# State-space sines one piece later, accumulated low parts from the 21st chunk with the negated copy first, and tiles moved in SBUF

## The chip, the cores and the metric

The kernel runs on one core of a Trainium2 chip. The time is the device time of one execution in microseconds; several executions are summed up by their median. TensorE (PE) multiplies, VectorE (DVE), ScalarE (ACT) and GpSimd (POOL) do the elementwise work, SyncE (SP) issues most DMAs; each takes its instructions strictly in the order in which they stand in the program.

## What is computed

One block of a decoder on 512 tokens with 2048 channels, all in float32:

```python
h = h + token_mixer(rmsnorm(h, norm_tok))     # one projection w_in to u, v, gates, merge gates;
                                              # state space, short convolution, w_glu, w_ssm_out,
                                              # w_conv_out, sigmoid merge, w_o
h = h + conv_ffn(rmsnorm(h, norm_ffn))        # w_up to 2 x 5632, convolution of 3 taps, gelu, w_down
return rmsnorm(h, norm_final)
```

The state space `s5_scan` has 32 pairs of groups; for each the kernel makes cosines and sines of phases, a product, two scans, a turn back and another product.

## The kernel before

**Products in three parts.** A float32 product is made of three `float32r` products: with hi the rounded value and lo what is left, it is hi·xh + hi·xl + lo·xh. The weights stand still in TensorE (128 x 128 at a time), the activations move, 512 columns (all tokens) or 256 (half of them). `products` issues the three matmuls for each of 8 blocks of a chunk: lines 161 (hi with xh), 162 (hi with xl) and 163 (lo with xh).

**Chunks.** The weights come in chunks of 128 x 1024 (8 blocks). The list `flat` holds all chunks in order, each with its unit (one output tile of 128 channels). A chunk passes through `load_to` (SyncE loads it to one of 3 `wraw` buffers) and `prep_to`, which makes its two parts in one of 3 `whi` and one of 3 `wlo` buffers. ScalarE copies to `whi` (line 138). The low part is made in one of two ways: by VectorE, `wlo = wraw - whi` (line 125), or, for units with `acc` set, ScalarE writes the rounded and negated `wraw` to `wlo` (line 141), and a DMA from GpSimd's queue adds `wraw` to it in SBUF (line 142). `acc` is set for the chunks from `flat[6:]` to the 20th merge unit, and of those a chunk goes to VectorE all the same when the count of background pieces left is 2 modulo 3.

**Order around a chunk.** When the products of chunk i stand in the program, `after(i)` issues, in this order: the two parts of chunk i + 3 (its buffers become free with chunk i), stores that were put off (`later`), loads up to chunk i + 5, then the next background pieces, then the hooks, then the unit's own end (`done`).

**Background pieces.** `bg_pieces(n)` makes three pieces for each n, which are taken one per chunk from the chunk 12 on, two per chunk in every fourth merge unit: `first` (the sum `ssm_y`, the sines `ssm_trig(n-1)`, the product `ssm_out`, the turn `ssm_turn(n-3)` on GpSimd, the scan of one half), `second` (the scan of the other half), `third` (a load, the product `ssm_bu`, the phases `ssm_phase(n)` on VectorE, lines 443 to 446, which write `ph`). `ssm_trig` is three ScalarE instructions (lines 452 to 454) that read `ph` and write `cs`; the scan and the turn read `cs`.

**The stages.** Chunks 0 to 15 are the state-space input u (each u tile is split to `uh` and `ul`, one buffer each, and stored by SyncE); 16 to 63 are the convolution's v, c and b gates; 64 to 127 the merge gates ("merges"); then w_conv_out (moving tile kh/kl), w_glu (xh/xl), w_ssm_out (kh/kl) and w_o (xh/xl), all with 512 columns. The two first units of w_up, `ua` and `ub`, move x2h/x2l with 512 columns; the other 43 pairs of w_up units (`Pair`) are computed with 7 chunks instead of 8 by sums of weights, with 256 columns: chunks 0, 3, 4, 5 move x2h/x2l, chunks 1 and 2 th/tl, chunk 6 the tile `xga`. w_down moves th/tl and x2h/x2l with 512 columns, its last 4 output tiles in two halves of 256.

**Where tiles lie.** Pools stack their tiles from the left or the right end of SBUF, so an address follows from the sizes of all tiles before it. Only its place within 256 bytes matters here:

| tile | before | with the change |
|---|---|---|
| whi, wlo | 192 | 192; 128 in units with `off` |
| xh, xl | 192 | 192 |
| kh, kl | 224 | 192 |
| x2h, x2l, xga | 224 | 128 |
| th, tl | 192 | 128 |
| ust and bst (state space) | 224 | 192 |

Of the kernel before, what the change touches and what calls it, by code (L numbers as in the profile page):

```python
# [16 lines left out]
P = 128  # L17
# [9 lines left out]
HALVES = (slice(0, T // 2), slice(T // 2, T))  # L27
SPLIT = 4

MAGIC = 12582912.0  # L30
# [18 lines left out]
class Unit:  # L49
# [7 lines left out]
    def __init__(self, chunks, xs, done, pre=None, bg=0, hooks=None, cols=slice(0, T), late=False, post=None):  # L57
        self.chunks, self.xs, self.done, self.pre, self.bg = chunks, xs, done, pre, bg
        self.hooks, self.cols, self.late, self.post = hooks or {}, cols, late, post
        self.total = sum(c[1] for c in chunks)  # L60
        self.k, self.ps = 0, None
        self.acc = False


@with_exitstack
def block_kernel(ctx: ExitStack, tc: tile.TileContext, a: dict):
# [5 lines left out]
    dpool = ctx.enter_context(tc.tile_pool(name="dpool", bufs=1, space=DRAM))  # L72
    psm = ctx.enter_context(tc.tile_pool(name="psm", bufs=3, space=PSUM))
    ctx.enter_context(tc.manual_schedule())

# [52 lines left out]
    def prep_to(n, late=False):  # L128
        while n_["prep"] < min(n, len(flat)):
            i = n_["prep"]  # L130
            load_to(i + 1)
            u, c = flat[i]
            w = slice(0, u.chunks[c][1] * P)
            raw = raws.pop(i) if i in raws else u.raw(c)
            hi = wpool.tile([P, 1024], F32R, tag="whi", name="whi")
            lo = wpool.tile([P, 1024], F32R, tag="wlo", name="wlo")
            preps[i] = (hi, lo)
            nc.scalar.activation(hi[:, w], raw[:, w], AF.Copy)  # L138
            if getattr(u, "acc", False) and len(bg) % 3 != 2:

                nc.scalar.activation(lo[:, w], raw[:, w], AF.Copy, scale=-1.0)
                nc.gpsimd.dma_start(lo[:, w], raw[:, w], accum_op=ALU.add)
                n_["prep"] += 1
                continue
            los.append((lo[:, w], raw[:, w], hi[:, w].bitcast(F32)))
            if not late:
                lo_all()
            n_["prep"] += 1
# [69 lines left out]
    def kd_chunks(w, n):  # L218
        return [(w[2 * n], 8), (w[2 * n + 1], 8)]
# [288 lines left out]
    def bg_pieces(n):  # L508

        def ok(p):  # L510
            return 0 <= p < NPAIR

        def quad(m):
            return m % 4 == 3 and ok(m)

        def first():
            if quad(n - 6):
                ssm_y((n - 6) // 4)
            if ok(n - 1):
                ssm_trig(n - 1)  # L520
            if quad(n - 5):
                ssm_out((n - 5) // 4)
            if ok(n - 3):
                ssm_turn(n - 3)
            if ok(n - 2):
                ssm_scan(n - 2, 0)

        def second():
            if ok(n - 2):
                ssm_scan(n - 2, 1)  # L530

        def third():
            if quad(n - 4):
                ur_load((n - 4) // 4)
            if ok(n - 1):
                ssm_bu(n - 1)
            if ok(n):
                ssm_phase(n)
                ssm_load(n + 1)
        return [first, second, third]  # L540
# [108 lines left out]
    add(*merges)  # L649
    for u, _ in flat[6:]:  # L650
        u.acc = u not in merges[20:]
# [6 lines left out]
    def start():  # L658
# [11 lines left out]
        raw = wpool.tile([P, 1024], F32, tag="wraw", name="wraw")  # L670
        hi = wpool.tile([P, 1024], F32R, tag="whi", name="whi")
        lo = wpool.tile([P, 1024], F32R, tag="wlo", name="wlo")
        half = [slice(0, 512), slice(512, 1024)]
# [173 lines left out]
    def sumsq(i, cols=slice(0, T)):  # L847
        h = hrow(i, cols)
        if i == 0:
            nc.scalar.activation(acc[:, cols], h, AF.Square)  # L850
            return
        ff["sq"] = fx("sq", (P, T), bufs=2)
        nc.scalar.activation(ff["sq"][:, cols], h, AF.Square)  # L853
# [42 lines left out]
    def gate_open():  # L896
        xctx.close()
        ff["gp"] = ctx.enter_context(tc.tile_pool(name="gp", bufs=1, side="left"))
        ff["pss"] = ctx.enter_context(tc.tile_pool(name="pss", bufs=5, space=PSUM))
        ff["TH"], ff["TL"] = (gt(t, 1, (P, KS, T), F32R) for t in ("th", "tl"))  # L900
        ff["pad"] = gt("ap", 1, (P, T + 2))
# [87 lines left out]
    class Pair:  # L989

        late = True
        pre = post = None

        def __init__(self, G):
# [106 lines left out]
    pairs = {G: Pair(G) for G in range(1, NG)}  # L1101
    ua, ub = (Unit(kd_chunks(a["w_up"], KF * r + ORDER[0]), xs2, f(ORDER[0])) for r, f in ((0, fa_done), (1, fb_done)))
    ua.pre = gate_open
    ua.hooks = {0: [f_sums, lambda: t_sums(KD - 1), lambda: s_first(1)], 1: [f_spread, t1_split, lambda: s_copy(1)]}
# [66 lines left out]
    for b_, (k0, kn) in enumerate(DOWN):  # L1171
# [3 lines left out]
        def down(n, **kw):  # L1175
            return Unit([(a["w_down"][n][:, k * P:(k + m) * P], m) for k in range(k0, k0 + kn, m)],
                        lambda k, k0=k0: xsd(k0 + k), dn_done(n, last, **kw), late=bool(kw), **kw)

        dns = [down(n) for n in range(KD - SPLIT if last else KD)]
        if not last:  # L1180
# [3 lines left out]
            for j in range(n1):  # L1184
                dns[3 + j].hooks.setdefault(0, []).append(lambda k=k1 + j: dg_split(k))
        add(*dns)
        if last:
# [5 lines left out]
            ends[SPLIT + 2].post = lambda: out_store(0, 4, 8)  # L1193
            add(*ends)

# [69 lines left out]
```

## Time and profile before

| | us |
|---|---|
| median of 3 runs | 2573.52 (2573.16 to 2574.19) |
| the profiled execution's own time | 2575.06 |
| its span, first to last instruction | 2573.3 |
| TensorE busy | 2520.0 (98%) |
| VectorE busy | 1670.1 (65%) |
| ScalarE busy | 1058.2 (41%) |
| GpSimd busy | 575.3 (22%) |
| granted TensorE clock, mean | 0.993 |

Times in rows are microseconds from the start of the span. Matmuls are pipelined: the mean ns of one in a row is longer than the distance from one start to the next, so the pace is read as the length of a stretch over the count of matmuls in it. PE is TensorE's matmuls, PEld its weight loads, SPq the queue of SyncE.

### The profile page before, as it was taken

What the parts mean: (1) busy time and instruction counts of PE and PEld (TensorE: products, weight loads), DVE (VectorE), ACT (ScalarE), POOL (GpSimd) and SP (SyncE); (2) the same over time, 40 slices, a digit from 0 to 9 for tenths busy, and PEclk for the clock granted to TensorE, in tenths of its full rate; (3) what the DMA queues carried; (4) which work ended last, traced back from release to release, by engine and by line L of the source; (5) the groups of instructions that cost most, each with busy time, mean ns of one, the idle gap of its engine ahead of it and who ended that gap; (6) DMA issues with size and microseconds to landing.
All of it is one profiled execution on the core that took longest, in us unless ns stands there. A gap on an engine that the chain in (4) does not pass through costs nothing.

```text
span 2573.3 us, 36516 instructions
## 1 busy us (share of the span) xinstructions
PE 2520.0 (98%) x14616; PEld 2204.6 (86%) x14616; DVE 1670.1 (65%) x1967; ACT 1058.2 (41%) x1343; POOL 575.3 (22%) x443
## 2 busy tenths in 40 slices
PE   9899999989999999999999999999999999999997
PEld 7678887767888888888999999999999988888887
DVE  6388889999323455446777777787777753333335
ACT  6344444444223433334544544555554432222222
POOL 2167777676202121110000000000000000000011
PEclk9999999999999999999999999999999999999998
DMA  7876777677445334443666666666666663434335
GB/s 218 240 175 182 192 205 192 172 188 192 141 149 191 123 127 141 145 144 123 169 182 179 169 164 177 190 185 172 170 181 175 195 238 112 126 112 123 97 92 152
DMA packets 151066, 424.70 MB, mean 165 GB/s; under 512 B 18032, under 2 KB 26352, under 8 KB 150896
## 3 DMA queue, kind: packets, MB, share of 16 engines
q1 hardware_dynamic: 121648, 330.88, 40.7%
q0 software_dynamic: 22176, 80.75, 16.5%
q10 hardware_dynamic: 7072, 10.74, 1.2%
q8 instruction: 114, 1.87, 0.3%
q14 instruction: 56, 0.46, 0.1%
HBM read 300.67 MB, written 40.89 MB: 133 GB/s over the span
## 4 chain that ended last, share of the span: by engine, by line
PE 86%; DMA 4%; issue 4%; DVE 3%; POOL 2%; ACT 1%; SPq 0%; ACTq 0%; DVEq 0%; POOLq 0%
PE mm L163 18%; PE mm L161 18%; PE mm L162 17%; PE sr L1021 11%; PE sr L1019 11%; PE sr L1020 11%; DMA wlo<-wraw 2%; POOL pt L94 1%; DVE wlo L125 1%; PE py L492 1%; DMA wraw<-in_w_in 1%; POOL xx L94 0%; DMA wraw<-wraw 0%; POOL xx L484 0%; PE w L461 0%
## 5 line engine op out<-in xcount | busy, mean ns | idle before, releaser
L125 DVE TENSOR_TENSOR wlo<-wraw,whi 128x1024 fp32r<-128x1024 f32 (+1 forms) x384 | 467.4, 1217 | 387.8 <-ACT whi L138 387.5
L138 ACT ACTIVATE whi<-wraw 128x1024 fp32r<-128x1024 f32 (+1 forms) x452 | 454.0, 1006 | 514.7 <-PE mm L162 389.1
L163 PE MATMUL mm<-xh,wlo 128*128 128x512 f32 x1344 | 529.9, 394 | 28.7 <-DMA wlo<-wraw 26.3
L161 PE MATMUL mm<-xh,whi 128*128 128x512 f32 x1344 | 529.6, 394 | 5.8 <-ACT whi L97 5.8
L162 PE MATMUL mm<-xl,whi 128*128 128x512 f32 x1344 | 527.7, 393 | 0.2 <-DVE xl L102 0.2
L1021 PE MATMUL sr<-x2h,wlo 128*128 128x256 f32 x1376 | 386.8, 281 | 1.4 <-DVE wlo L125 1.4
L1019 PE MATMUL sr<-x2h,whi 128*128 128x256 f32 x1376 | 385.5, 280 | 0.6 <-ACT whi L138 0.6
L1020 PE MATMUL sr<-x2l,whi 128*128 128x256 f32 x1376 | 382.8, 278 | 0.0
L163 PEld LDWEIGHTS mm<-xh,wlo 128*128 128x128 f32 x1344 | 254.9, 190 | 89.6 <-DMA wlo<-wraw 32.2
L161 PEld LDWEIGHTS mm<-xh,whi 128*128 128x128 f32 x1344 | 254.9, 190 | 66.2 <-issue 6.1
L162 PEld LDWEIGHTS mm<-xl,whi 128*128 128x128 f32 x1344 | 254.9, 190 | 55.0 <-DVE xl L102 1.4
L1021 PEld LDWEIGHTS sr<-x2h,wlo 128*128 128x128 f32 x1376 | 258.3, 188 | 2.2 <-DVE wlo L125 2.0
L1019 PEld LDWEIGHTS sr<-x2h,whi 128*128 128x128 f32 x1376 | 258.8, 188 | 0.8 <-ACT whi L138 0.8
L1020 PEld LDWEIGHTS sr<-x2l,whi 128*128 128x128 f32 x1376 | 258.8, 188 | 0.0
L163 PE MATMUL mm<-x2h,wlo 128*128 128x512 f32 (+1 forms) x528 | 197.8, 375 | 0.9 <-DVE wlo L125 0.9
L161 PE MATMUL mm<-x2h,whi 128*128 128x512 f32 (+1 forms) x528 | 198.5, 376 | 0.1
L162 PE MATMUL mm<-x2l,whi 128*128 128x512 f32 (+1 forms) x528 | 197.3, 374 | 0.0
L1021 PE MATMUL sr<-th,wlo 128*128 128x256 f32 x688 | 194.8, 283 | 0.9 <-DVE wlo L125 0.9
L1020 PE MATMUL sr<-tl,whi 128*128 128x256 f32 x688 | 194.7, 283 | 0.0
L1019 PE MATMUL sr<-th,whi 128*128 128x256 f32 x688 | 194.6, 283 | 0.0
L855 POOL TENSOR_TENSOR acc<-acc,sq 128x512 f32<-128x512 f32 (+1 forms) x31 | 37.6, 1214 | 655.0 <-ACT sq L853 655.0
L125 DVE TENSOR_TENSOR wlo<-r,whi 128x1024 fp32r<-128x1024 f32 x88 | 107.5, 1222 | 46.7 <-ACT whi L138 46.7
(246 smaller groups left out, 4534.3 us busy)
## 6 DMA issues: line engine op xcount, KB each, us to landing
wraw<-in_w_in SPq DMA_DIRECT2D x127, 512.0 KB, 4.3
r<-in_w_up SPq DMA_DIRECT2D x88, 512.0 KB, 6.1
xgb<-in_w_up SPq DMA_DIRECT2D x84, 512.0 KB, 5.5
wraw<-in_w_down SPq DMA_DIRECT2D x104, 384.0 KB, 3.3
wlo<-wraw POOLq DMA_DIRECT2D x68, 512.0 KB, 5.7
wraw<-wraw POOLq DMA_DIRECT2D x43, 512.0 KB, 9.6
wraw<-in_w_o SPq DMA_DIRECT2D x32, 512.0 KB, 3.6
r<-r POOLq DMA_DIRECT2D x22, 512.0 KB, 4.5
```

The source lines that it names most:

```text
L94: eng.tensor_tensor(o, x, y, op=ALU.mult)
L125: nc.vector.tensor_tensor(o, x, y, op=ALU.subtract)
L138: nc.scalar.activation(hi[:, w], raw[:, w], AF.Copy)
L161: nc.tensor.matmul(u.ps[:, u.cols], hi[:, w], xh, start=first, stop=False)
L162: nc.tensor.matmul(u.ps[:, u.cols], hi[:, w], xl, start=False, stop=False)
L163: nc.tensor.matmul(u.ps[:, u.cols], lo[:, w], xh, start=False, stop=last)
L492: nc.tensor.matmul(py[32 * q:32 * q + 32, :], cblk[:, p, j, :], xx[p][:, j], start=(j == 0), stop=(j == 1))
L855: nc.gpsimd.tensor_tensor(acc[:, cols], acc[:, cols], ff["sq"][:, cols], op=ALU.add)
L1019: nc.tensor.matmul(ps, hi[:, w], xh, start=(c < 4 and j == 0), stop=False, skip_group_check=c >= 4)
L1020: nc.tensor.matmul(ps, hi[:, w], xl, start=False, stop=False, skip_group_check=c >= 4)
L1021: nc.tensor.matmul(ps, lo[:, w], xh, start=False, stop=j == 7, skip_group_check=c >= 4)
```

## The change

Three things. First, `acc` is set from `flat[20:]` on, so that chunks 6 to 19 get their low part from VectorE, and where the low part is accumulated the negated copy to `wlo` stands ahead of the copy to `whi`. Second, `ssm_trig(n-1)` moves from piece `first` to the start of piece `second`. Third, tiles move: `whi` and `wlo` are 64 elements longer (`WT`), and a unit's `off` (0, or `SHIFT` = 48 elements, 192 bytes) says where in them its 1024 columns begin; `ua`, `ub` and all w_down units have the shift. A pool `edge` of 32 bytes at the right end, an `edge` tile of 192 bytes ahead of th and tl, and a single `sq` buffer of 528 instead of two of 512 elements set the places in the table above. In distances, 512-column products have weights and moving tile at the same place within 256 bytes throughout, and so do the 256-column products of w_down's last tiles; in the 43 pairs the weights lie 64 bytes beyond the moving tile.

```diff
+WT = 1024 + 64
+SHIFT = 48
...
-        self.acc = False
+        self.acc, self.off = False, 0
...
+    edge = ctx.enter_context(tc.tile_pool(name="edge", bufs=1, side="right"))
+    edge.tile([P, 8], F32, tag="edge", name="edge")
...
-            hi = wpool.tile([P, 1024], F32R, tag="whi", name="whi")
-            lo = wpool.tile([P, 1024], F32R, tag="wlo", name="wlo")
+            hi = wpool.tile([P, WT], F32R, tag="whi", name="whi")
+            lo = wpool.tile([P, WT], F32R, tag="wlo", name="wlo")
+            hi, lo = (x[:, u.off:u.off + 1024] for x in (hi, lo))
             preps[i] = (hi, lo)
-            nc.scalar.activation(hi[:, w], raw[:, w], AF.Copy)
             if getattr(u, "acc", False) and len(bg) % 3 != 2:

                 nc.scalar.activation(lo[:, w], raw[:, w], AF.Copy, scale=-1.0)
+                nc.scalar.activation(hi[:, w], raw[:, w], AF.Copy)
                 nc.gpsimd.dma_start(lo[:, w], raw[:, w], accum_op=ALU.add)
                 n_["prep"] += 1
                 continue
+            nc.scalar.activation(hi[:, w], raw[:, w], AF.Copy)
...
         def first():
             if quad(n - 6):
                 ssm_y((n - 6) // 4)
-            if ok(n - 1):
-                ssm_trig(n - 1)
...
         def second():
+            if ok(n - 1):
+                ssm_trig(n - 1)
             if ok(n - 2):
                 ssm_scan(n - 2, 1)
...
-    for u, _ in flat[6:]:
+    for u, _ in flat[20:]:
         u.acc = u not in merges[20:]
...
-        ff["sq"] = fx("sq", (P, T), bufs=2)
+        ff["sq"] = fx("sq", (P, T + 16))[:, :T]
...
         ff["pss"] = ctx.enter_context(tc.tile_pool(name="pss", bufs=5, space=PSUM))
+        gt("edge", 1, (P, 48))
...
+    ua.off = ub.off = SHIFT
...
+        def shifted(u):
+            u.off = SHIFT
+            return u
...
-        add(*dns)
+        add(*map(shifted, dns))
...
-            add(*ends)
+            add(*map(shifted, ends))
```

ScalarE in the stage of u, where chunks 9 to 12 are prepared, before (`ut`, `uh` are u tiles, `ns`, `sm` small tiles of the norm and the parameters):

```order
L559 ACTIVATE ut<-mm 128x512
L138 ACTIVATE whi<-wraw 128x1024
L141 ACTIVATE wlo<-wraw 128x1024
L97 ACTIVATE uh<-cv 128x512
L351 ACT_TABLE_LOAD
L351 ACTIVATE sm_sn<-sm_tau 128x32
L352 ACTIVATE sm_sh<-sm_tau 128x32
L138 ACTIVATE whi<-wraw 128x1024
L141 ACTIVATE wlo<-wraw 128x1024
L97 ACTIVATE uh<-ut 128x512
```

And with the change, where it reads line 150 for the copy to `whi` and line 101 for `uh`; the copies to `wlo` are gone here:

```order
L565 ACTIVATE ut<-mm 128x512
L150 ACTIVATE whi<-wraw 128x1024
L101 ACTIVATE uh<-cv 128x512
L357 ACT_TABLE_LOAD
L357 ACTIVATE sm_sn<-sm_tau 128x32
L358 ACTIVATE sm_sh<-sm_tau 128x32
L150 ACTIVATE whi<-wraw 128x1024
L101 ACTIVATE uh<-ut 128x512
```

VectorE at the same place, before:

```order
L287 TENSOR_SCALAR sm_tau<-sm_tau 128x32
L586 COPY rstd<-statb 128x512
L94 TENSOR_TENSOR cv<-cv,rstd 128x512 x2
L94 TENSOR_TENSOR ut<-ut,rstd 128x512 x2
L98 TENSOR_TENSOR ul<-cv,uh 128x512
L293 TENSOR_TENSOR xx<-io,sm_tauh 128x512
```

With the change the subtractions that make `wlo` (line 129 there) stand between them:

```order
L293 TENSOR_SCALAR sm_tau<-sm_tau 128x32
L129 TENSOR_TENSOR wlo<-wraw,whi 128x1024
L592 COPY rstd<-statb 128x512
L98 TENSOR_TENSOR cv<-cv,rstd 128x512 x2
L98 TENSOR_TENSOR ut<-ut,rstd 128x512 x2
L102 TENSOR_TENSOR ul<-cv,uh 128x512
L129 TENSOR_TENSOR wlo<-wraw,whi 128x1024
L299 TENSOR_TENSOR xx<-io,sm_tauh 128x512
```

ScalarE in the merges, one turn of the three pieces, before (`cs` are the sines, `mt` a merge gate on its way to DRAM, `bst` the state space's weights):

```order
L452 ACTIVATE cs<-ph 128x512
L453 ACTIVATE cs<-ph 128x512
L454 ACTIVATE cs<-cs,halfpi 128x512
L138 ACTIVATE whi<-wraw 128x1024
L595 ACTIVATE mt<-mm 128x512
L596 DMA md<-mt 128x512
L138 ACTIVATE whi<-wraw 128x1024
L141 ACTIVATE wlo<-wraw 128x1024
L438 ACTIVATE bst<-braw 128x256
```

With the change the copy of the chunk whose low part VectorE makes (line 150) stands ahead of the sines, and of the accumulated chunk the negated copy (line 145) ahead of the plain one:

```order
L150 ACTIVATE whi<-wraw 128x1024
L458 ACTIVATE cs<-ph 128x512
L459 ACTIVATE cs<-ph 128x512
L460 ACTIVATE cs<-cs,halfpi 128x512
L601 ACTIVATE mt<-mm 128x512
L602 DMA md<-mt 128x512
L145 ACTIVATE wlo<-wraw 128x1024
L146 ACTIVATE whi<-wraw 128x1024
L444 ACTIVATE bst<-braw 128x256
```

## Rows read from the trace of the kernel before

**Rows 1.** The page: busy us (share) xinstructions; the chain's shares by engine.
```profile
PE 2520.0 (98%) x14616; PEld 2204.6 (86%) x14616; DVE 1670.1 (65%) x1967; ACT 1058.2 (41%) x1343; POOL 575.3 (22%) x443
...
PE 86%; DMA 4%; issue 4%; DVE 3%; POOL 2%; ACT 1%; SPq 0%; ACTq 0%; DVEq 0%; POOLq 0%
```

**Rows 2.** Waits of TensorE, whole span: us in total, times, longest us.
```profile
PE mm L163 <- DMA wlo<-wraw: 26.3, 14, 3.8
...
PE sr L1021 <- DVE wlo L125: 2.3, 4, 0.9
```

**Rows 3.** Stretches, TensorE: window, us, busy (xmatmuls), clock; kh, kh, xh, x2h moving.
```profile
782.60:872.20 89.60, 89.60 (x385) 1.00 0.52 177
915.76:1005.36 89.60, 89.60 (x385) 1.00 0.41 129
1005.36:1179.48 174.12, 174.12 (x769) 1.00 0.44 144
2418.54:2519.34 100.80, 100.80 (x433) 1.00 0.35 94
```

**Rows 4.** The same of one pair: chunk 0, chunks 1 and 2, 3 to 6.
```profile
1308.05:1310.88 2.83, 2.83 (x26) 1.00 0.90 284
1310.88:1316.63 5.75, 5.75 (x50) 1.00 0.86 221
1316.63:1327.94 11.31, 11.31 (x98) 1.00 0.47 113
```

**Rows 5.** Stretches: us, then busy (x) of PE, PEld, DVE, ACT, POOL, clock, DMA.
```profile
41.85:138.06 96.21, 84.96 (x349) 67.66 (x348) 49.77 (x123) 37.81 (x49) 14.08 (x14) 0.95 0.84 221
149.42:159.48 10.06, 7.31 (x26) 5.56 (x25) 9.92 (x11) 2.85 (x5) 9.64 (x7) 0.83 1.01 224
418.32:428.54 10.22, 7.35 (x26) 5.55 (x25) 10.02 (x9) 2.75 (x5) 8.96 (x7) 0.83 0.93 202
401.50:655.37 253.87, 239.38 (x1056) 188.65 (x1054) 239.26 (x210) 108.05 (x146) 177.98 (x128) 0.99 0.72 189
```

**Rows 6.** Waits of ScalarE from 41.85 to 149.4 us, the longest.
```profile
ACT uh L97 <- DMA uhl<-uh: 37.1, 6, 10.6
```

**Rows 7.** Waits of SyncE's queue from 41.85 to 149.4 us, the longest.
```profile
SPq L118 <- DMA wlo<-wraw: 69.2, 12, 11.7
```

**Rows 8.** VectorE's subtractions from 41.85 to 138.06 us: busy, mean ns, idle before.
```profile
L125 DVE TENSOR_TENSOR wlo<-wraw,whi 128x1024 fp32r<-128x1024 f32 x2 | 2.4, 1223 | 0.3 <-ACT whi L138 0.3
```

**Rows 9.** Waits of ScalarE in the merges, 401.5 to 655 us, the longest.
```profile
ACT cs L452 <- DVE ph L446: 96.0, 14, 10.9
```

**Rows 10.** Waits of TensorE in the merges, 401.5 to 655 us, the longest.
```profile
PE mm L163 <- DMA wlo<-wraw: 12.3, 7, 2.9
```

**Rows 11.** Instructions in time, merges: start, us, engine, line, tiles, [idle before <-releaser].
```profile
412.11 0.64 ACT L452 ACTIVATE cs<-ph 128x512 f32<-128x512 f32 x1 [7.53 <-DVE ph L446]
...
414.91 1.06 ACT L138 ACTIVATE whi<-wraw 128x1024 fp32r<-128x1024 f32 x1 [0.41 <-ACT mt L595]
...
415.88 1.04 ACT L141 ACTIVATE wlo<-wraw 128x1024 fp32r<-128x1024 f32 x1
...
417.22 0.88 POOL L142 DMA_DIRECT2D wlo<-wraw  x1 [2.12 <-ACT bst L438]
...
421.80 0.50 PE L163 MATMUL mm<-xh,wlo 128*128 128x512 f32 x1 [2.87 <-DMA wlo<-wraw]
```

**Rows 12.** Instructions in time in one pair, from the end of its chunk 0.
```profile
1310.89 0.28 PE L1019 MATMUL sr<-th,whi 128*128 128x256 f32 x1
...
1311.09 0.39 ACT L1028 ACTIVATE t<-sr 128x256 f32<-128x256 f32 x1 [1.77 <-PE sr L1021]
...
1315.86 0.75 DVE L1053 SCALAR_TENSOR_TENSOR cv<-ap,vec,cv 128x512 f32<-128x512 f32 x1
...
1318.26 1.22 DVE L125 TENSOR_TENSOR wlo<-xgb,whi 128x1024 fp32r<-128x1024 f32 x1 [0.54 <-ACT whi L138]
...
1319.71 0.28 PE L1021 MATMUL sr<-x2h,wlo 128*128 128x256 f32 x1
```

## What the change was predicted to do

> **What bounds the kernel now.** I read the shares first, then who waits for whom, then the pace of TensorE stage by stage. TensorE is busy 98% of the span and holds 86% of the chain that ended last [rows 1], so only two things can move the time: the places where it waits, and the time that one matmul takes from its start to the next one's. By far the largest wait is that of the third product for the low part `wlo`, which a DMA from GpSimd's queue accumulates: 26.3 us in 14 pieces [rows 2]. The pace is read from stretches without a wait, length over matmuls: 174.12 us for 768 matmuls of 512 columns with xh moving is 226.7 ns; 89.60 us for 384 with kh is 233.3 ns, twice; 100.80 us for 432 with x2h is 233.3 ns [rows 3] (a row counts one more, at its edge). The same instruction is 6.6 ns slower where the moving tile starts 32 bytes off the weights' place in 256 bytes. With 256 columns it is the other way: 2.83 us for 24 with x2h (32 bytes off) is 117.9 ns, 5.75 us for 48 with th (in line) is 119.8 ns, 11.31 us for 96 with x2h and xga is 117.8 ns [rows 4].
>
> All sums are against the profiled execution, 2575.06 us with a span of 2573.3; the median of the runs, 2573.52, is 1.5 lower, and the forecast is brought down by that at the end. A measurement of this kernel can tell about 0.2%, 5 us, from no change.
>
> **Part 1: low parts of chunks 6 to 19 by VectorE.** These 14 chunks took 96.21 us [rows 5]. At 226.7 ns, 14 x 24 matmuls are 76.2 us, and the row's 13 others (norm, state space) at most 2.9: about 17.5 us are lost, part of it at the lower clock (granted 0.95). The rows show a loop. SyncE waits 69.2 us for `wlo` DMAs [rows 7], since a raw buffer is free only when its accumulation has landed; behind that load stand the stores of `uh`; ScalarE waits 37.1 us for those stores [rows 6]; behind it stand the next chunk's copies, and behind them the next accumulation. The change takes 12 accumulations and 12 negated copies out and puts 12 subtractions on VectorE, 1.22 us each [rows 8]: 14.7 us on top of 49.8 [rows 5], 64.5 in a stretch that would last 79, so 82% busy. What is queued behind a subtraction there is the small work of the parameters and the `ul` splits; TensorE needs a low part only two chunks (10.9 us) after its buffers are free. That cover would go if VectorE's backlog reached about 9 us. Bounds: 9 us gained (half stays, since `uh` has one buffer still and each chunk needs its store landed) and 17.5. I take 14, nearer the top, because the 12 waits of SyncE, which close the loop, go.
>
> **Part 2: the negated copy first.** For the 56 chunks that are still accumulated, the DMA is released one ScalarE copy earlier: 415.88 back to 414.91, 1.0 us in the example [rows 11]. The plain copy comes 1.0 us later; it is needed two chunks later, so that is hidden. Chunk 22 took 10.06 us rather than 5.5 [rows 5], 4.6 lost, the clock at 0.83 in it; with the low part 1 us earlier and less of a queue before it I take 2.5, bounds 0 and 4.6.
>
> **Part 3: the sines one piece later.** In the merges (401.50 to 655.37 us) TensorE waits 12.3 us for seven `wlo` DMAs [rows 10]; chunks 68 and 92 also lose the clock: 68 took 10.22 us, 4.8 more than 5.44, of which 2.9 is the wait [rows 5, 11]. So 12.3 + 2 x 1.9 = 16 us are lost. Rows 11 show how: ScalarE stands 7.53 us before `cs`, waiting for VectorE's `ph`; only then come the copies at 414.91 and 415.88, the DMA at 417.22, and TensorE goes on at 421.80. Such waits are 96.0 us in 14 pieces, 6.9 each [rows 9]. One piece later is usually one chunk, 5.4 us: 6.9 becomes 1.5. But `ph` itself is not earlier. Where it was ready two chunks late, the accumulated chunk gains only the plain copy that now stands ahead of the sines and the 1.0 us of part 2, 2 us together; seven waits of 12.3 us are 1.8 each, so most go and the longest (2.9) stay in part. What is late next is VectorE: it is busy 239.26 of 253.87 us here [rows 5], so the stretch can shrink by hardly more than 14.6 us whatever ScalarE does. GpSimd's turns, queued ahead of two of the seven DMAs, stay. Readers of `cs` (VectorE's scan, GpSimd's turn) come two pieces later and had three. Bounds 4 and 14.6; I take 11, six of seven waits at 1.8 each.
>
> **Part 4: 512 columns in line.** With kh 768 matmuls and with x2h in the down projection 1104 go from 32 bytes off to in line: 1872 x 6.6 ns = 12.4 us. All run at the head of the path. The 192 of the first two w_up units move too, but next to them TensorE waits for VectorE [rows 2], so I count none. The last 288 matmuls, of 256 columns, go in line and lose 288 x 1.9 ns = 0.5 us. One row bears on whether place matters at all: the 6.6 ns. The Trainium skill's page "SBUF — State Buffer", section "Who interferes with whom", gives TensorE two independent read ports and says that it never waits on anyone; by that rule no tile's place would matter and parts 4 and 5 would be nothing, 2546 us. Rows 3 speak against it.
>
> **Part 5: 256 columns, 64 bytes apart.** All 43 pairs of the up projection, 168 matmuls each, go to a distance that no row of before shows: weights 64 bytes beyond the moving tile. Now they average (5160 x 117.85 + 2064 x 119.8) / 7224 = 118.4 ns. From above the nearest row is th, in line, 119.8: 7224 x 1.4 = 10.1 us lost. From below it is half of the 512-column pace, 113.3: 36.8 us gained, less what VectorE takes back. In a pair, chunk 0 ends at 1310.89 and the low part of chunk 4 is done at 1319.48, 8.59 us later, through ScalarE's copy of `t`, VectorE's convolution and the copy after it; TensorE uses it at 1319.71 [rows 12]. At 113.3 ns three chunks take 8.16 us, and 0.2 us per pair come back as a wait, 8.6 in all: 28 gained. Neither end is nearer, so I take the middle, 116.6 ns: 7224 x 1.85 = 13.4 us gained, and three chunks of 2.80 us just cover the 8.59. The Trainium skill's page "TensorE: Matmul & The Clock Gate", section "Back-to-back issue gap", gives N / 2.4 + 2.5 ns; by it 256 columns would be 109.2 ns, an estimate that is 66 us less before any wait, but the 512 columns should then be 215.8 and the trace has 226.7.
>
> **The sum.** 14 + 2.5 + 11 + 12.4 - 0.5 + 13.4 = 52.8; 2575.06 - 52.8 = 2522.3, and 1.5 lower for the median: **2521 us**. Its own range, where the bounds of parts 1 to 3 and 115 to 118 ns in part 5 don't all fall on one side, is 2505 to 2540.
>
> **Rivals.** (1) *Own start, not distance.* The trace can't tell whether 32 bytes between the tiles count or the moving tile's start off a multiple of 64. If the latter, 512 columns gain as above and all 256-column matmuls go to 119.8 as th has it: 13.4 + 10.1 more, 2544. For it: th starts on such a multiple and is the slow one; against: nothing but that th is also the only tile in line. (2) *The floor*, 113.3 ns with VectorE's wait: 28 for 13.4, 2506. For it: at 226.7 ns per 512 columns TensorE takes columns that fast; against: none of the three rows of a pair [rows 4] is under 117.8. (3) *VectorE becomes the bound* in the early chunks and the merges: 9, 0 and 4 for 27.5, 2535 with the rest as it is, 2549 with part 5 at nothing. For it: 94% busy in the merges; against: 82% early. (4) *Placement does nothing*, 2546. (5) *Slower*: weights 64 bytes on cost the 256-column matmuls what 32 bytes cost the 512-column ones, 6.6 ns: 7224 x 6.6 = 48 lost in place of 13.4 gained, 2582. It decides from 5.4 ns on, where it eats the other parts' 39.4, above 123.8 ns. Against it: 32 bytes off made 256 columns faster, not slower.
>
> **How the numbers follow.** Forecast 0.50, own start 0.22, floor 0.13, VectorE 0.05, no effect 0.05, slower 0.05. To leave out no more than 2 in 10 the range takes in the own-start case with its early and merge bounds above and most of the floor's below: 2494 to 2550. Faster by over 0.2%: 0.94; within: 0.01; slower: 0.05.
>
> **What would show it.** Right: no wait of SyncE for `wlo` DMAs before chunk 20, chunks 6 to 19 within about 80 us; waits of ScalarE for `ph` in the merges well under 96 us; 384 kh matmuls in 87.0 us; 24 of a pair in 2.80 us, a pair in about 19.6 rather than 19.89. Wrong: a pair above 20.1 (own start) or near 21 (slower); TensorE waiting for VectorE's `wlo` where it waited for the DMA's (part 1 or 3); kh at 233.3 ns (part 4).

## The result, and the profile after

The changed kernel took **2549.73 us** (median; 2546.43 to 2549.99) beside 2573.60 for the kernel before on the same chip: a ratio of 0.9904, 95% interval 0.9887 to 0.9921. That is faster, at the upper edge of the range, but by 24 us where 52.5 were forecast. The profiled execution has a span of 2548.2 us, 25.1 less than before.

Busy time of the changed kernel and its chain of waits by engine, which answer to [rows 1]:

```profile
PE 2497.5 (98%) x14616; PEld 2195.8 (86%) x14616; DVE 1711.2 (67%) x1979; ACT 1048.8 (41%) x1331; POOL 559.5 (22%) x431
...
PE 80%; DMA 5%; DVE 5%; issue 4%; POOL 3%; ACT 2%; SPq 0%; ACTq 0%; DVEq 0%; POOLq 0%
```

TensorE is as full as it was, but its share of the chain fell from 86% to 80% and VectorE's rose from 3% to 5%: VectorE's work has come onto the path. Its 41 us of new busy time are more than the 14.7 of the 12 new subtractions. The waits of TensorE, as in [rows 2]:

```profile
PE mm L169 <- DMA wlo<-wraw: 20.9, 10, 4.4
PE mm L167 <- ACT whi L101: 5.7, 1, 5.7
PE mm L169 <- DVE wlo L129: 3.3, 4, 2.0
```

The stage windows of the changed kernel say where (columns as in [rows 5]): chunks 6 to 19, chunk 22, chunks 23 to 63, chunks 64 to 109, the first stretch with kh, and one with x2h in the down projection.

```profile
42.80:121.23 78.43, 78.43 (x349) 64.71 (x348) 62.88 (x131) 28.47 (x39) 4.32 (x3) 1.00 0.64 201
132.57:142.35 9.78, 7.32 (x26) 5.60 (x25) 9.68 (x7) 2.90 (x4) 8.59 (x7) 0.83 1.02 227
142.35:396.97 254.62, 243.23 (x1062) 194.78 (x1061) 238.34 (x210) 105.72 (x137) 178.83 (x130) 0.97 0.68 173
396.97:680.61 283.64, 274.48 (x1217) 217.76 (x1216) 248.76 (x223) 118.88 (x156) 188.19 (x131) 0.98 0.71 188
778.53:865.57 87.04, 87.04 (x385) 72.07 (x384) 38.85 (x39) 38.65 (x54) 28.21 (x19) 1.00 0.53 182
...
2395.65:2489.49 93.84, 93.84 (x416) 77.73 (x414) 34.91 (x35) 25.19 (x34) 12.95 (x10) 1.00 0.34 94
```

And the kernel before in chunks 23 to 63 and 64 to 109, a cut that the earlier rows don't have:

```profile
159.48:395.60 236.12, 236.12 (x1062) 191.01 (x1061) 207.30 (x208) 107.71 (x140) 188.67 (x131) 1.00 0.71 186
395.60:684.69 289.09, 274.60 (x1218) 216.39 (x1216) 251.25 (x220) 115.55 (x153) 187.25 (x131) 0.99 0.70 185
```

Chunks 23 to 63, for which the prediction counted nothing, took 18.5 us longer, with VectorE busy 238.3 us instead of 207.3 on the same instructions. Step by step, in us against the span of before ("pairs" is the stretch from chunk 208, the fifth of the first pair, to chunk 506; its last two chunks are w_down's first):

| step | predicted | measured |
|---|---|---|
| chunks 6 to 19 | -14 | -17.8 |
| chunk 22 | -2.5 | -0.3 |
| chunks 23 to 63 | 0 | +18.5 |
| chunks 64 to 109 (merges) | -11 | -5.4 |
| 512 columns in line | -12.4 | -14.3 |
| last halves | +0.5 | +0.5 |
| pairs | -13.4 | -7.6 |
| elsewhere | 0 | +1.3 |
| sum | -52.8 | -25.1 |

What happened in chunks 23 to 63 stands in two places of the timelines. Before (VectorE's `nk` and the next instruction, and the start of GpSimd's turn; start, us, engine, line, tiles):

```profile
183.93 0.43 DVE L445 TENSOR_SCALAR nk<-ph 128x512 f32<-128x512 f32 x1
184.39 0.69 DVE L446 TENSOR_TENSOR ph<-ph,nk 128x512 f32<-128x512 f32 x1
...
184.90 1.62 POOL L94 TENSOR_TENSOR xx<-zz,cs 128x512 f32<-128x512 f32 x1
```

And in the changed kernel, the same instructions of the same group:

```profile
169.74 3.48 DVE L451 TENSOR_SCALAR nk<-ph 128x512 f32<-128x512 f32 x1
173.26 1.64 DVE L452 TENSOR_TENSOR ph<-ph,nk 128x512 f32<-128x512 f32 x1
...
169.79 1.93 POOL L98 TENSOR_TENSOR xx<-zz,cs 128x512 f32<-128x512 f32 x1
171.04 1.89 POOL L98 TENSOR_TENSOR pt<-zz,cs 128x512 f32<-128x512 f32 x1
```

The turn used to start 0.97 us after `nk`; it now starts 0.05 us after it, and `nk` takes 3.48 us instead of 0.43: it ends 0.29 us after the second of GpSimd's two instructions. The turn stands in GpSimd's queue behind the accumulating DMAs, and these go out a copy earlier now.

### The profile page after: what moved, and what is told of

Read it like the earlier page. It is cut to its first block, busy times and chain, and to the rows that moved or that the text cites. A ratio compares the mean times of both kernels' runs of the same rounds, so it can differ in the third digit from the quotient of the medians.

```text
span 2548.2 us, 36443 instructions
## 1 busy us (share of the span) xinstructions
PE 2497.5 (98%) x14616; PEld 2195.8 (86%) x14616; DVE 1711.2 (67%) x1979; ACT 1048.8 (41%) x1331; POOL 559.5 (22%) x431
## 4 chain that ended last, share of the span: by engine, by line
PE 80%; DMA 5%; DVE 5%; issue 4%; POOL 3%; ACT 2%; SPq 0%; ACTq 0%; DVEq 0%; POOLq 0%
PE mm L169 18%; PE mm L167 18%; PE mm L168 18%; PE sr L1029 9%; PE sr L1027 8%; PE sr L1028 8%; DMA wlo<-wraw 2%; DVE wlo L129 2%; ACT whi L150 1%; DMA wraw<-wraw 1%; POOL pt L98 1%; POOL xx L98 1%; POOL xx L490 1%; PE py L498 1%; DMA th<-ghl 0%
## 5 line engine op out<-in xcount | busy, mean ns | idle before, releaser
L129 DVE TENSOR_TENSOR wlo<-wraw,whi 128x1024 fp32r<-128x1024 f32 (+1 forms) x396 | 479.7, 1211 | 368.8 <-ACT whi L150 368.3
L150 ACT ACTIVATE whi<-wraw 128x1024 fp32r<-128x1024 f32 (+1 forms) x396 | 395.3, 999 | 488.4 <-PE mm L168 391.5
```

The lines of the kernel that those rows point to most:

```text
L129: nc.vector.tensor_tensor(o, x, y, op=ALU.subtract)
```

## The experiments

**Undoing one part at a time.** In the first three runs one part of the change is taken back, in the fourth only the placement is left. The first puts the plain copy in front again:

```diff
+                nc.scalar.activation(hi[:, w], raw[:, w], AF.Copy)
                 nc.scalar.activation(lo[:, w], raw[:, w], AF.Copy, scale=-1.0)
-                nc.scalar.activation(hi[:, w], raw[:, w], AF.Copy)
```

> The changed kernel with one part undone: for the accumulated low parts the plain copy to whi stands ahead of the negated copy again. Chunks 23 to 63 took 236.1 us before and 254.6 with the change; VectorE's nk took 0.43 us in all 15 cases before, over 3 us in 7 with the change. Theory A (the negated copy first frees GpSimd's accumulations earlier, so its turn runs into VectorE's phases): chunks 23 to 63 fall back to about 237 us, nk to 0.43, time about 2532 us. Theory B (the early gain is only given back, since the state space's work is due anyway): no change, 2548 to 2551 us. Theory C (the sines' move does it): no change either, 2548 to 2551.

Measured: 2538.87 us, ratio 0.9853 (0.9836 to 0.9870). Chunks 23 to 63, then 64 to 109:

```profile
142.69:378.44 235.75, 235.75 (x1061) 191.13 (x1060) 206.97 (x208) 105.13 (x137) 188.14 (x131) 1.00 0.72 187
378.44:671.51 293.07, 277.26 (x1218) 218.98 (x1216) 247.46 (x220) 118.45 (x156) 188.03 (x131) 0.98 0.69 182
```

The 18.9 us are back, VectorE is at 207, and `nk` at 0.43 us in nearly all cases. But the merges lose 9.4 us against the changed kernel, so that the time is 7 us above the 2532 expected. The same edit costs 18.9 us in one stage and gains 9.4 in the next.

The sines in their old piece:

```diff
+            if ok(n - 1):
+                ssm_trig(n - 1)
             if quad(n - 5):
...
         def second():
-            if ok(n - 1):
-                ssm_trig(n - 1)
```

> The changed kernel with one part undone: the sines stand in piece first again. Theory A (negated copy): chunks 23 to 63 stay at 250 us or more; merges longer by up to 5 us, time 2550 to 2555 us. Theory B (backlog): the same. Theory C (the sines' move): chunks 23 to 63 back to about 237 us, time about 2532 us.

Measured: 2547.03 us, ratio 0.9885 (0.9871 to 0.9900); chunk 22, 23 to 63, 64 to 109:

```profile
131.69:137.13 5.44, 5.44 (x26) 4.51 (x24) 5.37 (x5) 2.83 (x4) 5.36 (x4) 1.00 1.03 239
137.13:393.57 256.44, 243.15 (x1061) 194.88 (x1060) 240.28 (x210) 105.51 (x137) 177.83 (x131) 0.97 0.69 173
393.57:680.21 286.64, 276.30 (x1217) 218.92 (x1216) 247.20 (x223) 117.94 (x156) 185.43 (x131) 0.98 0.70 186
```

The sines' move is not what costs the time in chunks 23 to 63. In the merges the stretch is 3.0 us longer without it, but that is less than the scatter: the nine runs here with late sines and the negated copy first in the merges took 280.3 to 285.8 us there. At chunk 22 the move costs 4.3: with the sines early the negated copy does cure that chunk, as the prediction had it, and the two parts of the change work against each other there. On the whole this run is no slower than the changed kernel, so no gain of the sines' move is shown.

Accumulated low parts from chunk 6 again:

```diff
-    for u, _ in flat[20:]:
+    for u, _ in flat[6:]:
```

> The changed kernel with one part undone: low parts are accumulated from chunk 6 on again. Chunks 6 to 19 back to about 96 us from 78.4 by every theory. Theory A and C: chunks 23 to 63 stay about 254 us, time about 2567 us. Theory B (what is gained early is lost later): chunks 23 to 63 fall back to about 236 us, time 2548 to 2551 us.

Measured: 2565.56 us, ratio 0.9960 (0.9947 to 0.9973). Chunks 6 to 19 take 95.23 us, chunks 23 to 63 the same 254.62 as with the change. So the early gain is not simply handed back later: theory B falls here.

The placement alone (the first, second and third edit together):

> The kernel before with the third part alone: tiles moved, copies, sines and low parts as before. In the changed kernel the stretches with kh took 5.2 us less, the pairs 7.5, the rest of w_up and the down projection 8.6. If the places alone do this: 21 less than before, about 2552 us, chunks 23 to 63 at 236. If places also matter to VectorE or GpSimd (nk at other addresses): chunks 23 to 63 near 254 us, about 2571 us.

Measured: 2550.25 us, ratio 0.9903 (0.9878 to 0.9928). Chunks 23 to 63 take 235.74 us, the kh stretches 87.04, the pairs 847.0: moving tiles is worth about 24 us (25.3 were forecast for parts 4 and 5) and leaves chunks 23 to 63 and the merges as they were. That is as much as the whole change gained (ratio 0.9904): what the other two parts gain in chunks 6 to 19 and in the merges they lose in chunks 23 to 63. Of the two runs with the plain copy first, this one, with early sines, needs 288.3 us in the merges, and the first, with late ones, 293.1; the 4.7 us between them, one run each, are again within the scatter of that stretch.

**Which order where.** The negated copy first for the merges alone:

```diff
-                nc.scalar.activation(lo[:, w], raw[:, w], AF.Copy, scale=-1.0)
-                nc.scalar.activation(hi[:, w], raw[:, w], AF.Copy)
+                both = [(hi, 1.0), (lo, -1.0)]
+                for o, s in both[::-1] if i >= 64 else both:
+                    nc.scalar.activation(o[:, w], raw[:, w], AF.Copy, scale=s)
```

> The changed kernel with the negated copy first only for the chunks of the merges, the plain copy first ahead of them. If the two orders act only where they stand: chunks 23 to 63 at 235.8 us as with the plain copy first, chunks 64 to 109 at 283.7 as with the change, 18.9 less than the changed kernel: about 2530 us. If the merges gain only because VectorE came into them with another backlog: merges near 293 us, about 2539 us.

Measured: **2529.20 us**, ratio 0.9828 (0.9810 to 0.9845), the lowest median here of a kernel that computes everything, 0.76% or some 20 us better than the changed kernel (called the best version below):

```profile
141.87:377.63 235.76, 235.76 (x1062) 190.97 (x1060) 207.09 (x205) 105.25 (x137) 188.89 (x131) 1.00 0.71 187
377.63:663.10 285.47, 275.04 (x1217) 217.81 (x1216) 250.75 (x223) 118.85 (x156) 186.77 (x131) 0.98 0.71 187
```

The orders act where they stand. Two attempts to save chunk 22 as well did not add up. The first:

```diff
+                for o, s in both[::-1] if i < 24 or i >= 64 else both:
...
-            if ok(n - 1):
+            if ok(n - 1) and n >= 17:
                 ssm_trig(n - 1)
```

(with the sines of the earlier groups in piece `first`)

> The changed kernel with the negated copy first only up to chunk 23 and in the merges, and the sines one piece later only from the merges on. In the run with the sines back chunk 22 took 5.4 us, in all others 9.7 to 12.0. Orders act only where they stand: chunk 22 at 5.4, chunks 23 to 63 at about 236, merges at 283.7, time about 2525 us. Otherwise chunk 22 stays near 10 us and the time near 2530.

Measured: 2533.23 us, ratio 0.9843 (0.9826 to 0.9859). Chunk 22 took 6.34 us, but chunks 23 to 63 took 242.94. The second, on top of the best version, accumulates only from chunk 24 on (`flat[24:]`):

> The kernel with the negated copy first in the merges alone, accumulating only from chunk 24 on. Chunk 22 took 9.9 us there, 4.5 over 5.44, TensorE waiting for an accumulated low part. If that wait is the DMA's: chunk 22 falls to about 5.4 to 6 us, chunks 23 to 63 stay at 236, time about 2525 us. If VectorE is already full there (91% busy from chunk 20 to 22): the loss stays or moves to the next chunks, 2528 us or more.

Measured: 2533.52 us, ratio 0.9834 (0.9818 to 0.9851); chunk 22, then 23 to 63:

```profile
131.55:136.99 5.44, 5.44 (x25) 4.50 (x24) 5.36 (x4) 1.04 (x1) 5.36 (x5) 1.00 0.55 169
136.99:382.17 245.18, 238.17 (x1061) 192.18 (x1060) 218.21 (x215) 107.04 (x140) 192.04 (x133) 0.99 0.69 181
```

The wait at chunk 22 is the DMA's, and it goes; but 9.4 us come back behind it, with VectorE at 218 us and one wait of TensorE for a `wlo` DMA of 5.3 us at 173 us. In this small form theory B is right: what VectorE has no time for here is paid a few chunks later. The intervals of both attempts overlap that of the best version, so by their times none of the three is ahead.

**Is it GpSimd's work beside VectorE?** First a small DMA ahead of each turn, to push it away from `nk`:

```diff
+        if p < 15:
+            nc.gpsimd.dma_start(pause, a["vec"][:, 0:32])
         t, z = cs.pop(p), zz.pop(p)
...
+    pause = dpool.tile([P, 32], F32, tag="pause", name="pause")
```

> The changed kernel, negated copy first everywhere, with one small DMA more (128 x 128 bytes, to a place that nothing reads) in GpSimd's queue ahead of each turn of the first 15 groups. Its issue takes up to about 0.9 us, so the turn starts later against VectorE's nk. Theory A in its narrow form (the turn starts 0.05 us after nk rather than 1.0 after it, and nk then stands 3.5 us): nk 0.43 us in nearly all, chunks 23 to 63 at about 236 to 240 us, about 2531 us. If the collision is not what costs the time: chunks 23 to 63 at 254 us or more, 2549 us or more.

Measured: 2543.63 us, ratio 0.9879 (0.9865 to 0.9894). `nk` fell to 0.43 us in most cases, but the turn now starts 0.61 us after it, and the instruction behind it, `ph`, took the blow: 32.0 us in 14 rather than 9.7. Chunks 23 to 63: 252.27. With two such DMAs:

> The same with two such small DMAs ahead of each turn. With one, the turn started 0.61 us after nk and it was the next instruction, ph, that stood: ph's 14 took 32.0 us rather than 9.7, nk's 10.0 rather than 6.1, and chunks 23 to 63 took 252.3 us. If an instruction of VectorE that starts after GpSimd's turn has begun is what stands: two issues move the turn to 1.1 to 1.2 us after nk, behind ph, both fall to about 6 and 10 us, chunks 23 to 63 to about 236 to 240, time about 2531. If the negated copy costs the time in another way: chunks 23 to 63 stay above 250 us.

Measured: 2538.72 us, ratio 0.9855 (0.9840 to 0.9871), but the profiled execution still has 252.79 us in chunks 23 to 63. A miss in the number that mattered. The timeline shows the blow moved once more, to the sum in the scan (0.69 us where nothing is beside it):

```profile
202.45 0.69 DVE L452 TENSOR_TENSOR ph<-ph,nk 128x512 f32<-128x512 f32 x1
...
203.16 1.95 POOL L98 TENSOR_TENSOR xx<-zz,cs 128x512 f32<-128x512 f32 x1
...
204.37 2.52 DVE L478 TENSOR_TENSOR zz<-zz,dt 128x512 f32<-128x512 f32 x1
```

Delaying the turn doesn't mend the rhythm: the blow moves on to VectorE's next instruction, and its sum over all of them stays high (230 us here). So the last test leaves the order as the change has it and takes GpSimd's work away:

```diff
             mul(x[:, j], z[:, j], t[:, 0], nc.gpsimd)
+            if p < 15:
+                continue
```

> The changed kernel; of GpSimd's turns of the first 15 groups only the first product of each half is computed, the second product and the sum are left out, so that GpSimd works a third as long beside VectorE in chunks 20 to 63. The copies, their order and the DMAs are those of the changed kernel. If VectorE is what runs late, held up by GpSimd's turn: VectorE's busy time in chunks 23 to 63 falls from 238 us to 205 or less, and the stretch from 254.6 to about 236 us. If the order of the copies costs the time by itself (the plain copy or the DMA at another moment): the stretch stays at 250 us or more although VectorE is freed.

Chunks 23 to 63 measured (the whole: 2523.54 us, with part of the work left out):

```profile
142.48:378.23 235.75, 235.75 (x1062) 190.96 (x1061) 182.31 (x209) 105.65 (x137) 89.21 (x77) 1.00 0.74 188
```

235.75 us, with the negated copy first throughout. The order of the copies costs nothing by itself; what costs is that it sets GpSimd's turn against VectorE. This run also empties GpSimd's own queue, in which the accumulating DMAs stand, but that queue was not what ran late: in the changed kernel GpSimd is idle for 4.2 to 8.5 us, waiting for VectorE, shortly ahead of four of the five late DMAs, and for 0.6 us ahead of the fifth, which makes TensorE wait 0.3 us.

**The pace of TensorE.** The matmuls alone, no other work beside them, all distances and four starts of the moving tile:

```diff
+    plan = [(c, (m + d) % 64, m) for c in (512, 256) for m in (0, 8, 16, 48) for d in range(0, 64, 8)]
+    for c, w, m in plan + plan[::-1]:
+        look(c, w, m)
```

> No part of the block is computed here: only matmuls, 96 in a row for each place, with 512 and with 256 columns, hi, hi, lo as in a chunk. The weights begin 0, 32, ... 224 bytes beyond the moving tile's place in 256 bytes, and the moving tile at four starts (0, 32, 64, 192 bytes more than 128). Distance theory: the pace goes by the distance alone: 512 columns 226.7 ns at distance 0 and 233.3 at 224 at each of the four starts, 256 columns 119.8 at 0, 117.8 at 224, and at 64 the 113.3 or 117.8 that the pairs show now. Own-start theory: it goes by the moving tile's start: 226.7 and 119.8 at the starts 0, 64 and 192, 233.3 and 117.8 at 32, whatever the distance.

Measured, with the moving tile 32 bytes off a multiple of 64, each row 96 matmuls; 512 columns at the distances 0, 32, 64, 128, 192 and 224:

```profile
199.86:221.65 21.79, 21.79 (x97) 18.02 (x96) 0.69 (x1) 0.00 (x0) 0.00 (x0) 1.00 0.00 1
221.65:244.04 22.39, 22.39 (x97) 18.04 (x96) 0.69 (x1) 0.00 (x0) 0.00 (x0) 1.00 0.00 0
244.04:266.44 22.40, 22.40 (x97) 18.05 (x96) 0.69 (x1) 0.00 (x0) 0.00 (x0) 1.00 0.00 1
288.92:311.23 22.31, 22.31 (x98) 18.08 (x97) 0.69 (x1) 0.00 (x0) 0.00 (x0) 1.00 0.00 1
333.63:355.62 21.99, 21.99 (x98) 18.03 (x97) 0.69 (x1) 0.00 (x0) 0.00 (x0) 1.00 0.00 1
355.62:378.02 22.40, 22.40 (x98) 17.99 (x96) 0.69 (x1) 0.00 (x0) 0.00 (x0) 1.00 0.00 1
```

21.79 / 96 = 227.0 ns in line, 22.4 / 96 = 233.3 at 32, 64 and 224 bytes; the other three starts differ by 0.2 ns at most (except the first 96 of all, in which the run begins). At 192 bytes it was 229.0 ns on the way up through the distances and 233.3 on the way down, at each start. The distance decides, the start doesn't, though some distances have two values, by the way through the plan. 256 columns at 0, 64 and 192 bytes, and 192 in another place of the run:

```profile
825.40:836.93 11.53, 11.53 (x99) 11.53 (x98) 0.43 (x1) 0.00 (x0) 0.00 (x0) 1.00 0.01 1
848.28:859.59 11.31, 11.31 (x98) 11.31 (x97) 0.42 (x1) 0.00 (x0) 0.00 (x0) 1.00 0.01 1
893.89:905.20 11.31, 11.31 (x98) 11.31 (x97) 0.42 (x1) 0.00 (x0) 0.00 (x0) 1.00 0.01 1
1291.71:1302.60 10.89, 10.89 (x99) 10.89 (x97) 0.42 (x1) 0.00 (x0) 0.00 (x0) 1.00 0.00 0
```

120.0 ns in line, 117.8 at 64 and at six of eight places with 192, 113.4 at the other two: there the same distance has two paces.

In the kernel, with 192 bytes in the pairs (on top of the best version; `off = 32` in `Pair`) and in line (`off = SHIFT`):

> The kernel with the negated copy first in the merges alone, and in the pairs the weights 192 bytes beyond the moving tile instead of 64. With the matmuls alone, 192 bytes went at 113.3 ns in 2 of 8 looks and at 117.8 in 6, 64 bytes at 117.8 in 8 of 8; in the kernel at 64 bytes about a quarter of the pairs' chunks go at 113.3. If 192 bytes hold the fast pace better: the pairs (chunks 208 to 506, 844 to 852 us in six runs at 64 bytes) below 840 us, time below 2525. If both are the same by chance: 844 to 852, about 2529. If worse: above 852.

> The same with the weights in line with the moving tile in the pairs too. Alone, 256 columns in line went at 120.0 ns in 8 of 8 looks, as th did before (119.8): the 7176 matmuls of chunks 208 to 506 at 120.0 give 861 us, some 865 with the waits, 15 to 20 more than at 64 bytes: about 2547 us. If in the kernel the other engines' traffic sets the pace: 844 to 852 us, about 2529.

Measured: 2535.47 us (ratio 0.9844, 0.9829 to 0.9859) and 2548.09 us (0.9892, 0.9876 to 0.9909); chunks 208 to 506:

```profile
1190.41:2043.98 853.57, 851.21 (x7178) 847.64 (x7177) 665.72 (x820) 426.49 (x519) 72.23 (x84) 1.00 0.67 183
...
1187.36:2056.16 868.80, 867.02 (x7178) 864.53 (x7177) 667.70 (x820) 426.16 (x519) 72.26 (x84) 1.00 0.66 180
```

853.6 and 868.8 us, beside 844.2 at 64 bytes and 858.0 before. Against weights in line, 64 bytes are worth 17 to 25 us in the pairs (844 to 852 in the runs with them), and 192 bytes are no better than 64.

Then whether a wait sets the pace. Four chunks in a row, with a ScalarE copy that TensorE should wait for:

> No part of the block is computed here: only matmuls of 256 columns at distances 0, 32, ... 224 bytes, four chunks of 24 in a row after each of 12 waits of different length (TensorE waits for a ScalarE copy), and another pair of tiles from chunk to chunk, as in the pairs. If the pace is a state that a disturbance sets and that then holds: at 64 and 192 bytes some chunks at 113.3 ns and others at 117.8, the same within a chunk; at 0 all at 120.0. If it goes by the distance alone: one pace for each distance, whatever the wait.

It did not tell: TensorE waited once, at the start. Without waits the pace held one value for each distance, 117.8 ns at 64 bytes. Mended, so that the copy cannot start before the last matmul ahead of it:

```diff
+                l = ws[:, wo:wo + P] if c == 3 and j == 7 or c + j == 0 and low else wl[:, w]
```

> No part of the block is computed here. In e12 TensorE never waited, since ScalarE's copy was done long before the weights were used. Here the last matmul of every fourth chunk reads the weights that ScalarE then rewrites, and the first or the third matmul of the next chunk waits for that: 24 waits for each distance. If a wait sets a pace that then holds, as after the waits of the pairs: at 64 bytes chunks at 113.3 ns in a part of the cases, 117.8 in the others, and one pace within a chunk; in line 120.0 throughout. If the pace goes by the distance alone and the pairs' 113.3 ns come from the traffic of the other engines: one pace for each distance, 117.8 at 64 bytes, also after a wait.

Waits of TensorE in this run, and one chunk of 24 matmuls each at 0, 64 and 192 bytes:

```profile
PE mm L85 <- ACT ws L77: 66.1, 96, 26.5
PE mm L88 <- ACT ws L77: 14.9, 76, 0.2
...
58.45:61.33 2.88, 2.88 (x27) 2.88 (x26) 0.42 (x1) 0.00 (x0) 0.00 (x0) 1.00 0.00 0
632.88:635.60 2.72, 2.72 (x26) 2.72 (x25) 0.42 (x1) 0.00 (x0) 0.00 (x0) 1.00 0.00 0
1772.43:1775.26 2.83, 2.83 (x26) 2.83 (x25) 0.42 (x1) 0.00 (x0) 0.00 (x0) 1.00 0.00 0
```

At 64 bytes all 96 chunks went at 113.3 ns (the waits inside them taken off), at 192 bytes 4 of 96, in line none. So at 64 bytes TensorE has two paces, 113.3 and 117.8 ns: behind a wait it falls into the fast one here and keeps it through the two or three chunks up to the next wait.

## Why the prediction was right or wrong

**Part 1 was right, a little short.** The 14 chunks took 78.4 us ("within about 80"), TensorE without a gap; the gain of 17.8 is just past the upper bound of 17.5, and with accumulation from chunk 6 again it is gone (95.2). VectorE is busy 62.9 of 78.4 us, 80%, as worked out (82). The loop did not go as a whole: before chunk 20 SyncE still waits 6.1 us for one `wlo` DMA, and now 29.6 us for VectorE's subtractions, but ScalarE's waits for the stores fell from 37.1 us [rows 6] to 14.0.

**Part 2 is where the prediction failed.** "The plain copy comes 1.0 us later ... that is hidden" held: TensorE never waits for a `whi` of chunks 23 to 63. What failed is "the DMA is released one ScalarE copy earlier", counted as a gain and no more. Behind that DMA in GpSimd's queue stands the turn, and it is released earlier too. The step that is missing is the one that follows the queue past the DMA: what starts sooner, and what does it meet? It meets `nk` and the `ph` behind it: in chunks 23 to 63 these two take 50.5 us of VectorE instead of 15.7. So a stretch that the prediction had at 0 took 18.5 us more, two thirds of the 27.7 that are missing from the forecast.

VectorE's lateness reaches TensorE by a chain. ScalarE's `cv` needs VectorE's `zp`, a product of GpSimd needs the `cv` that VectorE adds to, and behind that product in GpSimd's queue stands the accumulating DMA. First `zp` of chunk 26 before, then with the change `zp` of the same chunk, GpSimd's product, the DMA, and TensorE's wait for it:

```profile
178.43 0.66 DVE L94 TENSOR_TENSOR zp<-mm,mt 128x512 f32<-128x512 f32 x1
...
164.24 0.66 DVE L98 TENSOR_TENSOR zp<-mm,mt 128x512 f32<-128x512 f32 x1
...
167.40 1.30 POOL L98 TENSOR_TENSOR cv<-cv,rstd 128x512 f32<-128x512 f32 x1 [4.16 <-DVE cv L612]
168.64 1.76 POOL L147 DMA_DIRECT2D wlo<-wraw  x2
...
173.28 0.62 PE L169 MATMUL mm<-xh,wlo 128*128 128x512 f32 x1 [2.12 <-DMA wlo<-wraw]
```

TensorE began chunk 26 at 176.28 us before and at 159.12 with the change, so `zp` comes 2.2 us into it before and 5.1 with the change. Of the seven `zp` of these chunks five come 1.2 to 5.1 us later than before, counted from the chunk's start, and behind each of the five stands a wait of TensorE for a `wlo` DMA, 11.4 us together; the two that come on time have none. With the plain copy first, or with the thin turn, no `zp` is late and TensorE does not wait there; with the pauses five of seven are late again. The other 7.1 us are TensorE's own: its granted clock is 0.97 on the mean there instead of 1.00, and it is busy 243.2 us instead of 236.1. The trace of before could have warned: its `nk` takes 0.43 us in these chunks but about 1.4 in most cases of the merges, where it runs beside GpSimd. The products that read one operand from PSUM (`dt`) stand at 0.68 us before and after. The Trainium skill's page "SBUF — State Buffer", section "Who interferes with whom", the section that the prediction quoted for TensorE, says it for these two: VectorE, in its fast modes or with two inputs in SBUF, and GpSimd share one pair of ports, and who starts first holds it for the whole instruction. The rows agree that one shuts the other out: `nk` ends 0.29 us after GpSimd's second instruction. On who starts first they don't: `nk` is listed as starting 0.05 us ahead of the turn, in another place 0.51 us ahead (at 316.79 us, 4.00 us long), and yet it is VectorE that stands; where the turn starts 0.97 us after it, it takes 0.43.

**Part 3 had the wrong lever.** ScalarE's wait for `ph` in the merges fell from 96.0 us [rows 9] to 53.6, but the stretch gained 5.4 us rather than 11. With the sines late and the plain copy first the wait falls just as far, and the stretch is no shorter than before (293.1 us; 289.1). ScalarE's wait in the merges, with the change and with the plain copy first:

```profile
ACT cs L458 <- DVE ph L452: 53.6, 12, 8.8
...
ACT cs L458 <- DVE ph L452: 52.2, 10, 8.0
```

So the sines' move, from which half of the 2 us per accumulated chunk was to come ("so most go"), gains nothing there by itself. The copies' order is worth 9.4 us in the merges, clear of the 5.5 us by which that stretch scatters; for the sines' move, +4.7 us with the plain copy first and -3.0 with the negated copy, neither sign is shown. With both changed, the `wlo` DMAs are waited for in four places, 7.1 us, instead of seven with 12.3 [rows 10]. Why the longer ones stay is open.

**Part 4 was right.** The kh stretches take 87.04 us, 226.7 ns per matmul (87.0 was named). The gain is 14.3 instead of 12.4 because the count was short: w_down has 1200 such matmuls, not 1104 (0.6), the first two w_up units gain too (0.5), and the rest comes where chunks of th and x2h alternate in w_down. In the last halves +0.5 came as worked out.

**Part 5 had the right bounds and the wrong picture.** It took a middle of 116.6 ns; the chunks go at 113.3 or at 117.8 (2.72 and 2.83 us), by turns. The formula N / 2.4 + 2.5 ns, which the prediction took from the Trainium skill's page "TensorE: Matmul & The Clock Gate", section "Back-to-back issue gap", stands there for a matmul by itself and not for such a stream, so its 109.2 ns was no measure for this one. The fastest pace seen here is 113.3 ns. A chunk with a wait, a fast one and a slow one of the changed kernel:

```profile
1387.62:1390.72 3.10, 3.01 (x26) 2.82 (x25) 3.09 (x5) 1.06 (x2) 0.00 (x0) 1.00 0.12 21
1390.72:1393.44 2.72, 2.72 (x26) 2.72 (x25) 1.15 (x2) 2.28 (x3) 0.00 (x0) 1.00 0.26 96
1396.27:1399.10 2.83, 2.83 (x27) 2.83 (x25) 2.58 (x4) 0.82 (x1) 0.00 (x0) 1.00 0.94 310
```

90 of the 299 chunks are fast in the profiled execution. As the floor rival had it, VectorE's chain takes part of it back: a fast pair has one such wait and takes 19.45 us, a slow one 19.82, one of before 19.89. The rival's 0.2 us of wait per pair are 0.37 here. The best version has 195 fast chunks and 844.2 us in the pairs; the runs of this placement lie between 844 and 852, so the time of these kernels scatters by some us with how often the pace is fast. Of the 13.4 us forecast 7.6 came in the changed kernel.

**The rivals.** The own-start case named 2544 and the case that placement does nothing 2546, both near the time measured, but for reasons that did not hold: 256 columns did not go to 119.8, and 512 columns in line did go to 226.7. That their numbers fit is luck. VectorE as the bound (2535 to 2549) is the nearest in mechanism, with the place wrong: it was looked for in chunks 6 to 19 and in the merges, and it came between them, where VectorE had room (207 of 236 us) until GpSimd met it.

## What to carry to other kernels

An instruction moved earlier releases all that stands behind it in every queue: follow the queue to the next engine and ask what will now run side by side, even where both engines have room. Where two engines slow each other, compare the durations of the same instruction in several stages of the trace; two values for one shape are the warning. And an order that helps in one stage can be kept to that stage: the negated copy first in the merges alone is worth some 20 us over having it everywhere, 18.9 of them in chunks 23 to 63.

## What was not expected of the hardware

- The pace of a matmul goes by how far its weights begin from its moving tile, modulo 256 bytes, and not by where either begins: with 512 columns 226.7 ns in line, 232 to 234 at most other distances (at 192 bytes 229.0 in half the cases); with 256 columns 120.0 in line, 116.6 to 120.0 elsewhere, and 113.4 at 192 bytes in two of eight cases.
- At 64 bytes, 256 columns have two paces that hold by themselves: 113.3 ns behind a wait (96 of 96 chunks), 117.8 where there was none (48 of 48). In the changed kernel 33 of 42 pairs go fast behind the wait in their fifth chunk. What drops the pace again stays open: in the trace it falls as the second th chunk or the xga chunk begins, and in some pairs it comes back there without a wait.
- A VectorE instruction of 0.43 us took 3.48 us, to the end of the second of two GpSimd instructions, the first of which is listed as starting 0.05 us after it.
